# A two-layer hybrid decoder step, split into two token halves with the MLP of one half traced between the heads of the other

## The chip, the cores and the metric

The kernel runs on one core of a Trainium2 chip. The metric is the device time of one execution in microseconds (us), the median of several.

## The reference

One inference step of two layers for a prompt of 1024 tokens and eight sample tokens that attend to paged caches; the 1032 tokens share the weights. Model width 1024, MLP width 4096, all in float32.

```python
D_MODEL = 1024; SEQ = 1024; DEC_BATCH = 8; PAST_LEN = 512; D_FF = 4 * D_MODEL
def _diff_attn(q1, q2, ...):            # layer 0, heads A (4): differential attention
    p = probs(q1, k1) - lam * probs(q2, k2)
    return jnp.einsum('bhqk,bkhe->bqhe', p, v)
def _hgrn2_chunk(S, xs): ...            # layer 0, heads B (4): gated recurrence in chunks
def _fox_attn(q, fq, q_pos, k, v, fk, k_pos):   # layer 1, heads C (8): forgetting attention
    s = einsum(q, k) * DH_C ** -0.5 + fq - fk   # fq, fk: running sums of log forget gates
    p = softmax(where(mask, s, NEG)); return p @ v
def _mlstm_chunk(carry, xs): ...        # layer 1, heads D (4): recurrence with state C, n, m
...
# each layer: h = rmsnorm(x); heads(h @ w_in) ; x += heads @ w_out
#             x += relu(rmsnorm(x) @ w_up) ** 2 @ w_down ;   at the end a last rmsnorm
```

Both prompt heads are causal: a token needs only tokens before it, in attention and in the two recurrences. For the eight samples, heads A and C gather K, V (and for C the log forget values) of 512 past rows each through a page table, 4 pages of 128 rows; heads B and D take a state from memory and write a new one.

## The kernel before

Activations lie with the features on the 128 partitions and tokens along the free axis, so a projection is a weight block of 128 output features (`wh`, `wl`) against a block of tokens. Each float32 product is made of three TensorE matmuls of hi and lo parts (`mm3`, L119: `wh`·`xh`, `wh`·`xl`, `wl`·`xh`) over 8 or 4 blocks of 128 input features. The 1032 tokens are three blocks of 344 (`TB`), so a weight block of 1024 input features costs 72 matmuls and one of 512 (output projection and down projection) 36. `wsplit` brings each weight block once: one DMA on SyncE's queue into `wr` (L97), ScalarE copies it rounded into `wh` (L98), GpSimd subtracts into `wl` (L99). Each of `wr`, `wh`, `wl` has two buffers.

The program is traced in the order of the layers. Stage by stage, in the profile's time: input projection of the first heads; four diff heads with the other input projections as `fill` between their pieces; HGRN heads with the output projection as `fill`; the rest of the output projection and the whole MLP of layer 0 with six accumulators (793 to 1506); gates and projections of layer 1; eight fox heads with fill; mLSTM with the output projection as fill; the MLP of layer 1 (2197 to the end). `tick` hands out `fill` (dense work) and `back` (the samples' work) at a rate per piece of a head. In the head stages of diff and fox the dense work has one accumulator bank of PSUM (`acc1`, `acc4`), in HGRN and mLSTM two.

The framework's list scheduler fixes the order on each engine when the program is built; on the chip each engine takes its instructions in that order. Priority is the order of the trace.

The sample's work of layer 1 (`fox_sample`) is a chain: rows of q to DRAM and back as broadcasts (`dq`), 32 gathers of K pages (`dk`) with a multiply on GpSimd and a sum on VectorE each, 32 gathers of log forget values (`lgg`, copied to `lg` by GpSimd), a softmax, its probabilities through DRAM (`ps_c`, `pse`), then 32 gathers of V pages with a broadcast matmul (`selb`) and a VectorE reduction each. Before, it stands as `back` beside the fox heads, from head 2 on. `mlstm_sample` (`vrow_d`, `vb`, `Cs`, `qsd`) stands beside the mLSTM chunks.

Of the kernel before, what the change touches and what calls it, by code (L numbers as in the profile page):

```python
# [10 lines left out]
F32 = mybir.dt.float32  # L11
# [11 lines left out]
TB = 344  # L23
NTB = T // TB
# [31 lines left out]
class Step:  # L56


    def __init__(self, tc, ctx, I, O):
# [7 lines left out]
        self.A = ent(tc.tile_pool(name="A", bufs=1))  # L67
# [9 lines left out]
        self.idb = cp.tile([128, 128], BF16, name="idb")  # L77
        self.tri = cp.tile([128, 128], BF16, name="tri")
        self.rb = cp.tile([128, T], F32, name="rb")

        self.xs = self.dr.tile([128, KC, T], F32, name="xs")
        self.os = [self.dr.tile([8, 128, T], F32, name=f"os{i}") for i in range(2)]

    def pool(self, st, name, bufs=1, psum=False):
        kw = dict(space=bass.MemoryType.PSUM) if psum else {}
        return st.enter_context(self.tc.tile_pool(name=name, bufs=bufs, reuse_waits="tile", **kw))
# [35 lines left out]
    def project(self, ps, src, evict, m=128, w=None):  # L122

        h, l = w or self.wsplit(src, KC, m)
        for tb in range(NTB):
            sl = slice(tb * TB, (tb + 1) * TB)
            pt = ps.tile([128, 512], F32, name="acc", tag="acc")
            self.mm3(pt[:m, :TB], h, l, self.xh, self.xl, range(KC), sl, m)
            evict(pt[:m, :TB], sl)
            yield  # L130

    def project_rms(self, ps, src, evict, rms, w=None):

        h, l = w or self.wsplit(src, KC)
        pts = []
        for tb in range(NTB):
            pts.append(ps.tile([128, 512], F32, name="acc", tag="acc"))
            self.mm3(pts[tb][:, :TB], h, l, self.xh, self.xl, range(KC), slice(tb * TB, (tb + 1) * TB))
        rms()
        for tb in range(NTB):  # L140
            evict(pts[tb][:, :TB], slice(tb * TB, (tb + 1) * TB))

    def project_to(self, pool, ps, src, dst, scale=None, keep=None, done=None):

        nc = self.nc
        z = pool.tile([128, T], F32, name="z", tag="z", bufs=2)
        yield from self.project(ps, src, self.scaled(z, scale))
        if keep is not None:
            nc.gpsimd.tensor_copy(keep, z[:, NP:])
        nc.sync.dma_start(dst, z[:])  # L150
# [25 lines left out]
    def scaled(self, dst, scale=None):  # L176

        nc, rb = self.nc, self.rb
        m = dst.shape[0]

        def ev(p, sl):
            if scale is None:
                nc.vector.tensor_tensor(dst[:, sl], p, rb[:m, sl], op=ALU.mult)  # L183
            else:
                nc.vector.scalar_tensor_tensor(dst[:, sl], p, scale, rb[:m, sl], op0=ALU.mult, op1=ALU.mult)
        return ev


    def gain(self, x, n, gcol, hi, lo):
# [3 lines left out]
        for sl in [slice(tb * TB, (tb + 1) * TB) for tb in range(NTB)] if n == KC - 1 else [slice(0, T)]:  # L193
# [3 lines left out]
    def sumsq(self, pool, x, n, tags=(("sq", 1), ("ld", 2))):  # L197
        nc = self.nc
        if n == 0:
            self.sq = pool.tile([128, T], F32, name="sq", tag=tags[0][0], bufs=tags[0][1])  # L200
            nc.scalar.activation(self.sq[:], x, AF.Square)
        else:
            t = pool.tile([128, T], F32, name="sqt", tag=tags[1][0], bufs=tags[1][1])
            nc.scalar.activation(t[:], x, AF.Square)
            nc.vector.tensor_tensor(self.sq[:], self.sq[:], t[:], op=ALU.add)  # L205

    def rms(self, pool, ps, sq=None, t0=0, n=T):

        nc = self.nc
        sq = self.sq if sq is None else sq  # L210
        full, rest = divmod(n, 128)
        pt = ps.tile([128, 512], F32, name="acc", tag="acc")
        for c in range(full + 1):
            w = min(128, n - 128 * c)
# [3 lines left out]
        for w, cs in ((128, slice(0, full)), (rest, slice(full, full + 1))):  # L218
            nc.vector.tensor_scalar(v[:w, cs], pt[:w, cs], 1.0 / D, EPS, op0=ALU.mult, op1=ALU.add)
        h = pool.tile([128, 9], F32, name="rp", tag="rp")  # L220
        nc.gpsimd.memset(h[:], -0.5)
        nc.gpsimd.tensor_tensor(v[:, :full + 1], v[:, :full + 1], h[:, :full + 1], op=ALU.pow)
        for g in range(0, full + 1, 4):
            pt = ps.tile([128, 512], F32, name="acc", tag="acc")
            for j, c in enumerate(range(g, min(g + 4, full + 1))):
                w = min(128, n - 128 * c)
                d = pool.tile([128, 128], F32, name="rd", tag="rd", bufs=2)
                nc.vector.tensor_scalar(d[:, :w], self.ident[:, :w], v[:, c:c + 1], None, op0=ALU.mult)
                nc.tensor.matmul(pt[:, 128 * j:128 * j + w], lhsT=self.ones[:], rhs=d[:, :w], start=True, stop=True)  # L229
            w = min(512, n - 128 * g)  # L230
            nc.scalar.copy(self.rb[:, t0 + 128 * g:t0 + 128 * g + w], pt[:, :w])


    def head_norm(self, sm, po, pm, dst, gcol, gate, n, eps=None, thr=None):

        nc = self.nc
        sq = sm.tile([128, 512], F32, name="hsq", tag="hsq")
# [3 lines left out]
        rs = sm.tile([128, 512], F32, name="hrs", tag="hrs")  # L241
# [11 lines left out]
    def hgrn_gates(self, ph, ps, pr, first):  # L253

        nc, I = self.nc, self.I
        self.fS = self.dr.tile([4, 128, T], F32, name="fS")
        self.gS = self.dr.tile([4, 128, T], F32, name="gS")
# [12 lines left out]
        for h in range(4):  # L270
            z = ph.tile([128, T], F32, name="z", tag="z", bufs=2)
            if h:
                self.now(self.project(ps, I["w_in_e"][16 + h], self.scaled(z)))
            else:
                self.project_rms(ps, None, self.scaled(z), lambda: self.rms(ph, pr), w=first)
# [3 lines left out]
            nc.sync.dma_start(self.fS[h], g[:])  # L279
        for h in range(4):  # L280
            z = ph.tile([128, T], F32, name="z", tag="z", bufs=2)
            self.now(self.project(ps, I["w_in_e"][24 + h], self.scaled(z)))
# [3 lines left out]
            nc.sync.dma_start(self.gS[h], g[:])  # L286
# [10 lines left out]
    def hgrn_unit(self, h, u, ph, ps):  # L297
# [7 lines left out]
        us = slice(N * u, N * u + N)  # L305
        t512 = lambda name, bufs: ph.tile([128, N], F32, name=name, tag=name, bufs=bufs)
        c3 = lambda ap: ap.rearrange("p (c t) -> p c t", t=128)
        f, q, it = t512("hf", 4), t512("hq", 6), t512("hi", 2)
        nc.sync.dma_start(f[:], self.fS[h, :, us])
        nc.sync.dma_start(q[:], self.qbS[h, :, us])  # L310
        nc.sync.dma_start(it[:], self.ibS[h, :, us])
        k = t512("hk", 5)
        nc.scalar.activation(k[:], f[:], AF.Copy, scale=-1.0, bias=1.0)
        yield
        ir = ph.tile([128, nch, 128], F32, name="hir", tag="hir", bufs=6)
# [5 lines left out]
        AT = ph.tile([128, nch, 128], F32, name="hA", tag="hA", bufs=6)  # L321
# [7 lines left out]
        pe, pes = f[:], ph.tile([128, N], F32, name="hpe", tag="hpe", bufs=5)  # L329
# [27 lines left out]
        nc.sync.dma_start(gt[:], self.gS[h, :, us])  # L357
        yield
        S = ph.tile([128, nch - 1, 128], F32, name="hS", tag="hS", bufs=3)
        end = ph.tile([128, 128], F32, name="hE", tag="hE", bufs=4)  # L360
# [22 lines left out]
        nc.sync.dma_start(self.os[0][4 + h][:, us], ot[:])  # L383
        self.half_done += u == 0
# [15 lines left out]
    def hgrn_sample(self, ph, ps):  # L400

        nc, I, O = self.nc, self.I, self.O
        for t, src in ((self.qb_s, self.qbS), (self.ib_s, self.ibS), (self.fb_s, self.fS), (self.gb_s, self.gS)):
            nc.sync.dma_start(t[:].rearrange("p (h b) -> p h b", b=NS), src[:, :, NP:].rearrange("h p b -> p h b"))
        pt = ps.tile([128, 512], F32, name="pm", tag="m")
        nc.tensor.transpose(pt[:32, :128], self.ib_s[:], self.ident[:])
        ri = ph.tile([32, 128], F32, name="ri", tag="row32", bufs=2)
# [1178 lines left out]
```

## Time and profile before

| | |
|---|---|
| time, median of 3 runs | 2920.72 us (2918.53 to 2924.51) |
| profiled execution | 2922.06 us, of it 2920.2 us from the first to the last instruction |
| TensorE busy | 2789.4 us, 17340 matmuls, mean granted clock 0.969 |
| VectorE / ScalarE / GpSimd busy | 1279.9 / 893.0 / 787.4 us |
| DMA | 261.5 MB, mean 90 GB/s |

A matmul's busy time overlaps with the next one's, so the pace of TensorE is read from the distance of starts or from a chain of many matmuls. An idle time is what no matmul covers; a granted clock of 0.5 in a stretch is the lower of its two levels.

### The profile page before, as it was taken

The numbers are of one execution on the slowest core, as the hardware profiler recorded it, in microseconds if no ns is written. First come the engines' busy times: TensorE is split into PE (matmuls) and PEld (weight loads), VectorE is DVE, ScalarE is ACT, GpSimd is POOL, SyncE is SP. The second block draws the span as 40 slices with busy tenths as digits, with TensorE's granted clock in tenths as the row PEclk, the third lists the DMA queues.
The fourth block names the chain that finished last, engine by engine and source line by source line (L and its number), as shares of the span: only waits on it lengthen the run. The fifth ranks groups of instructions, "written<-read, shape, count | busy, mean of one in ns | idle before, by whom it ended". The sixth has DMA issues, their size and how long they took to land.

```text
span 2920.2 us, 43534 instructions
## 1 busy us (share of the span) xinstructions
PE 2789.4 (96%) x17340; PEld 2652.7 (91%) x17340; DVE 1279.9 (44%) x2499; ACT 893.0 (31%) x1548; POOL 787.4 (27%) x640
## 2 busy tenths in 40 slices
PE   8999899799999999999999989889999999999997
PEld 8988777698999999999999988777889999999997
DVE  5144855575622333223344546474453333223335
ACT  4143343212522222222232524353342222222223
POOL 2321720254322222222222244211242222221222
PEclk9999999799999999999999999988999999999998
DMA  3253653542211111111133443644331111111121
GB/s 141 96 162 104 185 143 122 170 124 81 76 55 44 40 47 49 54 47 37 55 116 126 129 142 110 153 143 135 104 98 48 37 48 51 51 48 37 47 62 66
DMA packets 149868, 261.50 MB, mean 90 GB/s; under 512 B 24358, under 2 KB 69190, under 8 KB 149666
## 3 DMA queue, kind: packets, MB, share of 16 engines
q1 hardware_dynamic: 149410, 258.64, 29.3%
q8 instruction: 137, 2.24, 0.3%
q0 software_dynamic: 256, 0.08, 0.2%
q14 instruction: 65, 0.53, 0.1%
HBM read 209.75 MB, written 48.92 MB: 89 GB/s over the span
## 4 chain that ended last, share of the span: by engine, by line
PE 82%; DMA 5%; DVE 5%; issue 4%; POOL 1%; ACT 1%; SPq 1%; DVEq 0%; POOLq 0%; ACTq 0%
PE acc L119 71%; PE po L573 2%; PE S L520 1%; PE S L517 1%; PE pm L557 1%; PE pm L338 1%; DMA dI<-irow 1%; DVE xl L195 1%; DMA kd<-out_ka 1%; DVE sq L205 1%; PE hms L240 1%; DMA kd<-out_kc 0%; DMA ol<-os 0%; PE pm L710 0%; PE acc L229 0%
## 5 line engine op out<-in xcount | busy, mean ns | idle before, releaser
L119 PE MATMUL acc<-xh,wh 128*128 128x344 f32 (+1 forms) x2808 | 915.1, 327 | 28.2 <-DVE z L183 17.1
L119 PE MATMUL acc<-xl,wh 128*128 128x344 f32 (+1 forms) x2808 | 906.9, 323 | 0.6 <-DVE xl L195 0.5
L119 PE MATMUL acc<-xh,wl 128*128 128x344 f32 (+1 forms) x2808 | 899.9, 322 | 3.8 <-POOL wl L99 3.8
L99 POOL TENSOR_TENSOR wl<-wr,wh 128x512 fp32r<-128x512 f32 (+1 forms) x284 | 504.1, 1775 | 1414.3 <-ACT wh L98 1413.6
L119 PEld LDWEIGHTS acc<-xh,wh 128*128 128x128 f32 (+1 forms) x2808 | 534.1, 190 | 39.9 <-DVE z L183 19.6
L119 PEld LDWEIGHTS acc<-xh,wl 128*128 128x128 f32 (+1 forms) x2808 | 532.4, 190 | 6.3 <-POOL wl L99 4.6
L119 PEld LDWEIGHTS acc<-xl,wh 128*128 128x128 f32 (+1 forms) x2808 | 533.7, 190 | 3.3 <-DVE xl L195 1.6
L98 ACT ACTIVATE wh<-wr 128x512 fp32r<-128x512 f32 (+1 forms) x284 | 228.2, 804 | 982.4 <-PE acc L119 843.9
L119 PE MATMUL acc<-ul,wh 128*128 128x344 f32 (+1 forms) x1568 | 495.8, 317 | 0.1
L119 PE MATMUL acc<-uh,wl 128*128 128x344 f32 (+1 forms) x1568 | 494.0, 317 | 1.5 <-POOL wl L99 1.5
L119 PE MATMUL acc<-uh,wh 128*128 128x344 f32 (+1 forms) x1568 | 493.2, 317 | 1.7 <-ACT wh L98 1.7
L1267 DVE TENSOR_TENSOR x<-acc,x 128x344 f32<-128x344 f32 x336 | 173.3, 516 | 438.3 <-PE acc L119 438.3
L119 PEld LDWEIGHTS acc<-uh,wh 128*128 128x128 f32 x1568 | 294.1, 188 | 2.2 <-ACT wh L98 2.1
L119 PEld LDWEIGHTS acc<-uh,wl 128*128 128x128 f32 x1568 | 293.7, 188 | 2.1 <-POOL wl L99 2.1
L119 PEld LDWEIGHTS acc<-ul,wh 128*128 128x128 f32 x1568 | 294.6, 188 | 0.6 <-DVE ul L1202 0.5
L1254 DVE TENSOR_TENSOR ul<-u,uh 128x344 fp32r<-128x344 f32 x192 | 146.1, 763 | 201.8 <-ACT uh L1253 201.8
L1251 DVE SCALAR_TENSOR_TENSOR t<-acc,rb 128x344 f32<-128x344 f32 x192 | 98.5, 516 | 268.1 <-PE acc L119 266.2
L1252 ACT ACTIVATE u<-t 128x344 f32<-128x344 f32 x192 | 93.8, 490 | 323.5 <-DVE t L1251 322.5
L183 DVE TENSOR_TENSOR z<-acc,rb 128x344 f32<-128x344 f32 x138 | 69.9, 512 | 207.6 <-PE acc L119 191.2
L539 ACT ACTIVATE e<-S,st 128x128 f32<-128x128 f32 (+7 forms) x128 | 94.4, 739 | 95.3 <-DVE st L537 42.7
L545 ACT ACTIVATE Ph<-pm 128x512 fp32r<-128x512 f32 (+1 forms) x120 | 64.8, 551 | 110.0 <-PE pm L557 109.1
L1253 ACT ACTIVATE uh<-u 128x344 fp32r<-128x344 f32 x192 | 94.0, 491 | 5.8
(385 smaller groups left out, 3259.0 us busy)
## 6 DMA issues: line engine op xcount, KB each, us to landing
wr<-in_w_up SPq DMA_DIRECT2D x64, 512.0 KB
wr<-in_w_down SPq DMA_DIRECT2D x128, 256.0 KB
wr<-in_w_in_e SPq DMA_DIRECT2D x27, 512.0 KB
wr<-in_w_out SPq DMA_DIRECT2D x48, 256.0 KB
wr<-in_w_in_o SPq DMA_DIRECT2D x24, 512.0 KB
x<-in_x SPq DMA_DIRECT2D x16, 516.0 KB
qd<-qS SPq DMA_DIRECT2D x32, 256.0 KB
dk<-in_cache_k_a SPq DMA_DIRECT2D x32, 256.0 KB
```

The lines of the kernel that those rows point to most:

```text
L98: nc.scalar.activation(h[:, :kk, :m], r[:, :kk, :m], AF.Copy)
L99: nc.gpsimd.tensor_tensor(l[:, :kk, :m], r[:, :kk, :m], raw(h[:, :kk, :m]), op=ALU.subtract)
L119: nc.tensor.matmul(out, lhsT=w[:, k, :m], rhs=a[:, sl], start=(n == 0), stop=(n == last))
L183: nc.vector.tensor_tensor(dst[:, sl], p, rb[:m, sl], op=ALU.mult)
L539: nc.scalar.activation(e[:, :L], S[:, :L], AF.Exp, bias=st[:, 0:1], scale=-1.0, accum_out=st[:, 1:2])
L545: nc.scalar.activation(ph[:, :n], pt[:, :n], AF.Copy)
L573: nc.tensor.matmul(o[:, 128:] if half else o, lhsT=w, rhs=parts[x][:, c:c + (128 if half else 256)], start=(j == 0 and n == 0), stop=(j == ...
L1251: nc.vector.scalar_tensor_tensor(t[:], pt[:, :TB], 0.0, self.rb[:, sl], op0=ALU.max, op1=ALU.mult)
L1252: nc.scalar.activation(u[:], t[:], AF.Square)
L1253: nc.scalar.activation(H[:, sl], u[:], AF.Copy)
L1254: nc.vector.tensor_tensor(L[:, sl], u[:], raw(H[:, sl]), op=ALU.subtract)
L1267: nc.vector.tensor_tensor(x[:, sl], pt[:, :TB], self.x[n][:, sl], op=ALU.add)
```

## The change

The tokens are two halves of 512 and 520 (`HW`), and blocks are one of 512 columns for half 0, two of 260 for half 1. The output projection, the MLP and layer 1's input projection of a half are one generator, `half()`, which yields after each block; the run traces a half's generator as `fill` between the heads of the other half. The sequence is: first projections for both halves; HGRN heads of half 0 with the remaining projections; diff heads of half 0; diff heads of half 1 and HGRN heads of half 1, with layer 0's `half(0, 0)` and the samples of diff and HGRN; then for each half u of layer 1: input projection, fox heads, mLSTM, with `half(0, 1)` between those of half 0 and `half(1, 0)` between those of half 1; last `half(1, 1)` alone. The weights of `half()` and of layer 1's input are therefore loaded and split twice. `fox_sample` moves from beside the fox heads to half 1's mLSTM stage, ahead of `mlstm_sample`. The dense work in the head stages has two accumulator banks (`accM`). The second score matmul of diff reads all 128 partitions instead of 64.

```diff
-TB = 344
-NTB = T // TB
+HW = (NP // 2, T - NP // 2)
+BLOCKS = (((0, 512),), ((0, 260), (260, 260)))
...
+    def half(self, layer, u, ps, pr, tp, alone=False):
...
+        for part in range(2):
...
+            for f in range(KC):
...
+                h, l = self.wsplit(I["w_out"][layer, part, f], 4)
+                for o, m in blocks:
+                    pt, sl = acc(), slice(o, o + m)
+                    self.mm3(pt[:, :m], h, l, oh, ol, range(4), sl)
+                    nc.vector.tensor_tensor(x[f][:, sl], pt[:, :m], x[f][:, sl], op=ALU.add)
+                    yield
...
+        for cc in range(8):
...
+                h, l = self.wsplit(I["w_up"][layer, 4 * cc + f], KC)
...
+                h, l = self.wsplit(I["w_down"][layer, cc, f], 4)
...
         if fox is None:
-            q2, k2 = Q1[hi], K2[hi]
+            K2 = hd.tile([128, nk], F32R, name="K2", tag="K2", bufs=2)
+            nc.gpsimd.tensor_tensor(K2[:], kd[:], raw(K1[:]), op=ALU.subtract)
+            q2, k2 = Q1, K2
...
-            pS, pm, acc = self.pool(st, "pS4", 2, True), self.pool(st, "pm4", 2, True), self.pool(st, "acc4", 1, True)
...
-                    self.back = (66 / 24, [self.fox_sample(hd, pm, pS)])
...
-            self.fill = (32 / 70, [self.out_a(1, ph, acc, self.xs), self.out_b(1, ph, acc)])
-            self.back = (10 / 48, [self.mlstm_sample(ph, pm, qkv)])
...
+            accM = self.pool(st, "accM", 2, True)
...
+            self.fill = (1.7, [self.half(0, 0, accM, accM, M)])
...
+                self.diff_half(1, hd, pm, pS)
...
+                self.fill = (1.4, self.fill[1])
+                self.back = (76 / 60, [self.hgrn_sample(ph, pm, pS), self.diff_sample(ph, pm, pS)])
+                self.hgrn_half(1, ph, pm, 3, 5)
...
+            for u in range(2):
...
+                    self.fill = (0, [self.half(u, 1 - u, accM, accM, M)])
...
+                self.fill = ((5.0, 2.4)[u], self.fill[1])
...
+                    self.fox_half(u, hd, pm, pS)
+                self.fill = ((1.7, 1.4)[u], self.fill[1])
...
+                    if u:
+                        self.back = (76 / 30, [self.fox_sample(ph, pm, pS), self.mlstm_sample(ph, pm, pS, qkv)])
+                    self.mlstm_prompt(u, ph, pm, qkv)
+                    self.drain("back")
...
+            self.now(self.half(1, 1, ps, pr, tp, alone=True))
```

How the change moves instructions, at three places. First TensorE at the end of the fox heads. Before, the last heads' scores (`S`, L517, L519, L520), transposes (`pm<-ident`, L557) and products with V (`po`, L573) and the sample's broadcasts (`selb`, L710) follow one another:

```order
L710 MATMUL pm<-PP,selb 128x512
L557 MATMUL pm<-ident,e 128x128 x4
L573 MATMUL po<-Ph,VV_18707 128x256
L557 MATMUL pm<-ident,e 128x128 x4
L573 MATMUL po<-Pl,VV_18707 128x256
L573 MATMUL po<-Ph,VV_18707 128x256
L573 MATMUL po<-Pl,VV_18707 128x256
L557 MATMUL pm<-ident,e 128x128 x3
L573 MATMUL po<-Ph,VV_18707 128x256
L517 MATMUL S<-K_19000,Q_18999 128x384
```

After the change the last head of half 1 stands among dense matmuls (L121, 512 columns):

```order
L598 MATMUL po<-Ph,VV_21302 128x256
L598 MATMUL po<-Ph,VV_21302 128x128
L121 MATMUL acc<-uh,wh 128x512
L598 MATMUL po<-Pl,VV_21302 128x128
L598 MATMUL po<-Pl,VV_21302 128x256
L121 MATMUL acc<-ul,wh 128x512
L121 MATMUL acc<-uh,wl 128x512
```

The dense work that had run out in this place before now lies between the pieces.

Second SyncE's queue at the gathers of the log forget values. Each gather is a DMA with five control rows around it. Before, weight loads (`wr`) and stores stand between every few of them:

```order
L653 DMA lgg<-in_cache_logf_c 128x8
L647 TENSOR_LOAD pages
L647 ISA x2
L97 DMA wr<-in_w_in_o 128x1024
L653 ISA
L653 DMA lgg<-in_cache_logf_c 128x8
L1130 DMA os_84<-ft 64x512
```

After the change 25 of the 32 follow one another (the last two and what comes behind are shown), with no weight load among them:

```order
L676 DMA lgg<-in_cache_logf_c 128x8
L670 TENSOR_LOAD pages
L670 ISA x2
L676 ISA
L676 DMA lgg<-in_cache_logf_c 128x8
L670 TENSOR_LOAD pages
L670 ISA x2
L99 DMA wr<-in_w_down 128x512 x4
```

The four weight loads behind them are the next that TensorE's dense work needs.

Third TensorE at the end of the mLSTM sample (`qsd`, `Cs`, L1054 before, L1095 after). Before, its matmuls lie in groups of four between output projection and chunks:

```order
L119 MATMUL acc<-oh_19510,wl 128x344
L1054 MATMUL pm<-qsd,Cs 128x1 x4
L934 MATMUL pm<-ident,mvt 128x128 x4
L940 MATMUL pm<-ident,mk_19443 128x128
L940 MATMUL pm<-ident,mk_19444 128x128
L972 MATMUL pm<-mvr,mP 128x129 x4
L1054 MATMUL pm<-qsd,Cs 128x1 x4
L119 MATMUL acc<-oh_19507,wh 128x344
```

After the change they stand in one piece, and `half(1, 1)`, which has the 260-column matmuls, begins behind them:

```order
L733 MATMUL pm<-PP,selb 128x512
L1061 MATMUL pm<-w_24643,sel 128x16 x2
L682 MATMUL pm<-ident,vsd 32x128
L1066 MATMUL pm<-ed,ones 128x32
L1040 MATMUL pm<-ident,mh 128x128 x4
L1095 MATMUL S<-qsd,Cs 128x1 x32
L1098 MATMUL S<-qn,ones 128x16 x2
L1108 MATMUL pm<-hsd,ident 128x32
L254 MATMUL hms<-hsq,ones 128x32
L121 MATMUL acc<-uh,wh 128x260
```

No dense matmul is left between the last broadcast of the fox sample (`selb`) and the end of the mLSTM sample.

In the order after the change, 279 dense matmuls of 512 columns stand between the first matmul of the fox sample (a transpose of `qc_s`) and the `hms` above: 207 of them ahead of its softmax's scores, 72 behind; 142 rows of other matmuls stand among them. The stages with heads and fill (HGRN and diff of both halves; fox and mLSTM of each half) hold 3,724 dense matmuls of 512 columns and 2,210 of 260. Over the whole program, 4,728 dense matmuls have 512 columns and 9,456 have 260; before, the same 14,184 products were in three blocks of nearly always 344.

## Rows read from the trace of the kernel before

**Rows 1.** The page: busy time, share of the span and count of each engine.

```profile
PE 2789.4 (96%) x17340; PEld 2652.7 (91%) x17340; DVE 1279.9 (44%) x2499; ACT 893.0 (31%) x1548; POOL 787.4 (27%) x640
```

**Rows 2.** Stretches, all work: length, busy time of each engine, clock, DMA share, GB/s.

```profile
150.00:722.00 572.00, 525.02 (x3054) 456.22 (x3054) 343.85 (x779) 189.58 (x346) 188.20 (x172) 0.93 0.46 136
1590.00:2122.00 532.00, 484.08 (x2968) 428.74 (x2967) 283.81 (x631) 207.66 (x416) 149.97 (x176) 0.93 0.47 134
1865.00:1924.00 59.00, 58.52 (x382) 54.61 (x380) 33.08 (x78) 25.76 (x49) 11.10 (x12) 1.00 0.45 136
1924.00:1987.00 63.00, 51.88 (x261) 38.72 (x260) 42.97 (x97) 33.88 (x70) 2.90 (x11) 0.84 0.36 114
2122.00:2197.00 75.00, 71.66 (x470) 67.19 (x470) 45.10 (x65) 34.13 (x46) 30.69 (x22) 1.00 0.30 93
```

**Rows 3.** Chain that ended last: start, length, what, count; two dense pieces.

```profile
738.42 8.91 PE acc L119 x72
...
793.78 710.91 PE acc L119 x4512
```

**Rows 4.** Stretches, L119 alone: length, PE busy (count), weight loads, clock, DMA, GB/s.

```profile
150.00:722.00 572.00, 282.18 (x1528) 254.67 (x1528) 0.93 0.46 136
1590.00:2122.00 532.00, 275.11 (x1530) 250.30 (x1529) 0.93 0.47 134
1865.00:1924.00 59.00, 39.89 (x228) 36.13 (x226) 1.00 0.45 136
1924.00:1987.00 63.00, 0.08 (x1) 0.00 (x0) 0.84 0.36 114
```

**Rows 5.** TensorE's timeline between two dense blocks in the fox stage.

```profile
1677.42 0.31 PE L119 MATMUL acc<-xh,wl 128*128 128x344 f32 x1
1678.34 0.43 PE L119 MATMUL acc<-xh,wh 128*128 128x344 f32 x1 [0.61 <-DVE z L183]
```

**Rows 6.** TensorE's timeline: scores of a diff head; output projection with 512 columns.

```profile
204.73 0.50 PE L520 MATMUL S<-K,Q 64*128 64x512 f32 x1
205.16 0.44 PE L517 MATMUL S<-K,Q 128*128 128x384 f32 x1
...
705.06 0.39 PE L119 MATMUL acc<-ob,wl 128*128 128x512 f32 x1
705.29 0.40 PE L119 MATMUL acc<-ob,wh 128*128 128x512 f32 x1
```

**Rows 7.** Groups with shapes apart: busy us, mean ns, idle before, releaser.

```profile
L99 POOL TENSOR_TENSOR wl<-wr,wh 128x512 fp32r<-128x512 f32 x168 | 220.0, 1310 | 794.2 <-ACT wh L98 793.8 <-PE acc L119 0.4
L98 ACT ACTIVATE wh<-wr 128x512 fp32r<-128x512 f32 x168 | 105.8, 631 | 555.9 <-PE acc L119 534.8 <-issue 17.6 <-POOL wl L99 2.2
```

**Rows 8.** ScalarE's copies L98 from 2122 to 2146: what ended its idle times.

```profile
  PE acc L119: 8.3, 5
  DMA wr<-in_w_out: 0.5, 1
```

**Rows 9.** fox_sample, multiplies, copies, V reductions: ns min/median/max, first and last start.

```profile
L684 POOL TENSOR_TENSOR dk<-dk,dq x32: 1253/1288/1647, 1718.0 to 1785.3; 128x512 f32<-128x512 f32 x32
...
L1146 POOL COPY lg<-lgg x32: 192/198/424, 1786.5 to 1824.0; 128x8 f32<-128x8 f32 x32
...
L712 DVE CUSTOM_DVE_ANT_0 dk<-dk,pm x31: 668/681/689, 1857.7 to 1958.8; 128x512 f32<-128x512 f32 x31
```

**Rows 10.** Chain, fox and mLSTM sample: start, length, what.

```profile
1806.23 0.33 SPq L653
1807.39 0.33 SPq L653
...
1839.91 7.42 DMA ps_c<-de
1848.26 7.87 DMA pse<-ps_c
...
2019.78 5.13 DMA vb<-vrow_d
```

More of the change, by code (lines that the diff above doesn't have):

```diff
@@ new lines, in project_to @@
+    def project_to(self, pool, ps, src, dst, us=(0, 1), scale=None, keep=None):
+        nc = self.nc
+        t0, t1 = HS[us[0]].start, HS[us[-1]].stop
+        z = pool.tile([128, t1 - t0], F32, name="z", tag="z", bufs=2)
+        ev = self.scaled(z, us, scale)
+        h, l = self.wsplit(src, KC)
+        for u in us:
+            for _ in self.project(ps, None, ev, (u,), w=(h, l)):
+                yield
+            nc.sync.dma_start(dst(u), z[:, HS[u].start - t0:HS[u].stop - t0])
+        if keep is not None and t1 == T:
+            nc.gpsimd.tensor_copy(keep, z[:, NP - t0:])
@@ L835, in mlstm_rows @@
[L835 to L847 removed]
+        rs = slice(128 * h, 128 * h + 128)
@@ L908, in mlstm_prompt @@
[L908 to L913 removed]
+            pt = ps.tile([128, 512], F32, name="pm", tag="m")
+            nc.tensor.matmul(pt[:], lhsT=self.sel2[:, i, :], rhs=wi[:], start=True, stop=True)
+            nc.vector.tensor_tensor(qw[i][:], q[i][:, :512], pt[:], op=ALU.mult)
@@ new lines, in half @@
+            if cc == 7:
+                break
+            for f in range(KC):
+                h, l = self.wsplit(I["w_down"][layer, cc, f], 4)
+                for o, m in blocks:
+                    pt, sl = acc(), slice(o, o + m)
+                    self.mm3(pt[:, :m], h, l, uh, ul, range(4), sl)
+                    nc.vector.tensor_tensor(x[f][:, sl], pt[:, :m], x[f][:, sl], op=ALU.add)
+                    yield
+        if alone:
+            self.finish(tp, ps, pr, u, x, uh, ul, wd)
+            return
@@ new lines, in half @@
+        while layer == 0 and self.inp is None:
+            yield "wait"
+        ih, il, sq = [], [], None
+        for f in range(KC):
+            h, l = self.wsplit(I["w_down"][layer, 7, f], 4)
+            for o, m in blocks:
+                pt, sl = acc(), slice(o, o + m)
+                self.mm3(pt[:, :m], h, l, uh, ul, range(4), sl)
+                nc.vector.tensor_tensor(x[f][:, sl], pt[:, :m], x[f][:, sl], op=ALU.add)
+                yield
+            if layer == 0:
+                nc.sync.dma_start(self.xs[u][:, f, :], x[f][:, :n])
+                ih.append(self.inp.tile([128, n], F32R, name=f"ih{f}"))
+                il.append(self.inp.tile([128, n], F32R, name=f"il{f}"))
+                self.gain(x[f], f, C_MIX + 8, u, ih[f], il[f])
+            sq = self.sumsq(mp, x[f][:, :n], f, sq)
```

919 lines of the change are left out of this document (454 added, 465 removed).

## The prediction

> **What bounds the kernel now.** I read the page first: TensorE is busy for 2789.4 of 2920.2 us [rows 1], so only its work or its waits can give time back. Next the chain: from 793.78 on 4,512 dense matmuls take 710.91 us, 157.6 ns each [rows 3]. The two MLPs run at that pace without waiting, so nothing is to be had there. Then the stretches. The head stages, 150 to 722 and 1590 to 2122, are 1104 us long with TensorE idle for 47.0 and 47.9 us, and a granted clock of 0.93 [rows 2]; 7% of 1104 is 77 us that the lower of the two clock levels took. Together 172 us. The timeline shows that idle time is under-reported: between two dense blocks the starts are 0.92 us apart where the pace is 0.16, so 0.76 is lost and 0.61 shown, while the only bank is emptied by `z` [rows 5]. Scaling the 95 us by that quarter gives 119, and 196 us lost in all, 18% of these stages.
>
> What do they depend on? L119 counted alone has 1,528 and 1,530 matmuls there [rows 4], at 157.6 ns 482 us, 44% of the time. Where dense work is 61% (228 matmuls in 59 us, 1865 to 1924), 0.5 us is idle at full clock, a loss of 1%; where there is none (1924 to 1987) 11.1 us is idle and the clock is 0.84, a loss of about a third [rows 2, 4]. Waits of heads are lost when the fill is thin or has run out. That is what the change moves.
>
> **The sum.** Dense work: a weight block took three blocks of 344, 472.7 ns per product of 128 by 128; now one of 512 and two of 260. 512 columns start 0.23 us apart [rows 6]. For 260 a line through the two paces gives 121 ns, the chain of 72 gives 123.8 with whatever it waited [rows 3]. So 0.23 + 2×0.121 is 472 ns, no change; with 123.8 it is +5 ns, over 4,728 products +23 us. I take +10 (0 to +23); this also stands for the doubled weight stream, of which below.
>
> Scores: 64-row matmuls of 512 columns are followed after 0.43 us, where 128 rows take 0.23 [rows 6]. By the order there are 48 of 512 columns and 48 of fewer; 96 by about 0.19 saved is −18. The 32 additional transposes of V, at about 0.22, cost 7. Together −11 (−18 to 0).
>
> Joints: where heads ended and the MLP began, 3.3 of 75 us are idle [rows 2]; two such joints now lie beside heads: −6 (−8 to 0).
>
> Head stages: their other work is 1104 − 196 − 482 = 426 us, 415 after the line above. By the order, 3,724 × 0.23 + 2,210 × 0.121 = 1124 us of dense work stand there, 73% of 1539. That is above the 61% stretch, with two banks, but holds over a much longer time, with each head's loads and set-up twice. From 1% (that stretch) to 10% (halfway to today's 18%) I take 4%: 62 us lost instead of 196, −134 (−181 to −42).
>
> The new hole: `fox_sample` now stands at the end, and `half(1, 0)` does not last as long as it. Its chain worked out: q rows to DRAM and back 8 us (as `ps_c`, 7.4 [rows 10]); the K multiplies 41 at GpSimd's 1.29 each, 69 as they ran before (1718.0 to 1786.6), I take 55 [rows 9]; then copies of log forget values, the last 37 us after the last multiply [rows 9], which is also 32 gathers at SyncE's 1.16 apart [rows 10]; softmax with two trips through DRAM, 7.4 and 7.9 [rows 10], some 18; V 37 at the gathers' pace, up to 60, I take 50 (101 before, spread by its rate [rows 9]); `mlstm_sample`, eight states in two buffers, four rounds of `vb` at 5.1 [rows 10] and about 1.5 of arithmetic, with a trip for its rows and its tail 35 (30 to 45). Sum 203 us (169 to 237). Beside it TensorE has 279 dense matmuls, 65 us, and 142 rows of other work, an estimate of 45: 110. What is left is a wait of 93 us; I take +90 (59 to 127). What is late next: 25 gathers in a row on SyncE take 29 us, and the weight loads behind them (`in_w_down`) come that much later, so dense work can't fill the time; on TensorE everything queues behind the waiting scores, then behind `S<-qsd,Cs`, and `half(1, 1)` begins only after the `hms` that follows.
>
> The moved gathers of layer 0 I cost at nothing: diff and HGRN samples have over 200 us of dense work and four head units beside them. Without that cover their chain is as long as the one above, less the log forget values.
>
> Sum against the profiled execution: 2922 + 10 − 11 − 6 − 134 + 90 = 2871; the median of the runs is 1.3 below it, so I say **2870**.
>
> The weight stream: a 256 KB block now serves 12 × 0.23 = 2.8 us of TensorE instead of 5.7. Copy and subtraction take 0.63 and 1.31 [rows 7]; with two `wr` buffers a load may take 5.6 − 0.63 − 1.31 = 3.6 us before TensorE waits. From 2122 on the output projection already ran at one block per 2.9 us; ScalarE waited there five times for TensorE (8.3 us) and once for the load (0.5) [rows 8]. So on a quiet memory it is hidden. The Trainium skill's "DMA: Bandwidth & Descriptors", section "Anatomy of one DMA", speaks against halving what a load serves: each DMA has a fixed part of about 2.0 us that does not shrink with its size. By its formula 256 KB is 2.6 us (an estimate from that page), below the 3.6, and the dense term would be 0 and the sum 2861.
>
> **The rivals.** *The hole is covered.* If K runs at GpSimd's pace and V at the gathers', the wait is 59, and with 1% of loss the head stages give 181: 2922 + 10 − 11 − 6 − 181 + 59 = 2793, with single terms between 2780 and 2830. For it: the 61% stretch. Against: 25 gathers in a row.
>
> *The weight stream becomes the bound (slower).* Place: dense blocks of 512 words per partition in the mixed stages, where the DMA share is 0.46 [rows 2], against 0.30 in the stretch of rows 8. If a load takes 4.4 us there, two weights need 6.3 instead of 5.6, 0.37 us for each of 320 such blocks, +119 us at most: 2870 + 119 is about 2990, half of it 2930. It decides from 3.6 us on. For it: GpSimd gets about 400 us more of subtractions (144 more of 512 words at 1.31 [rows 7], 88 of twice that), and a `wl` stuck behind a sample's multiplies delays TensorE. The Trainium skill's "GPSIMD Engine Reference", section "Specifications", adds that GpSimd shares its SBUF interfaces with VectorE, with contention where a VectorE instruction has two inputs there. The multiplies' median and maximum, 1.29 and 1.65 [rows 9], would fit that. Against: rows 8, and that head work in between gives loads more time.
>
> *The waits belong to the heads, not to thin fill (slower).* Twice the units with shorter pieces wait twice as often; if 10% of 1539 is lost, −42 instead of −134: 2963. For it: 44% of dense work does not keep 18% from being lost today. Against: the single bank is gone.
>
> *It doesn't do what it says.* The scheduler could have pulled dense work together ahead of the heads, and gain and hole cancel: 2916 to 2927. The order, which has dense rows between head pieces, speaks against it.
>
> **How the numbers follow.** Chances: the sum 0.50 (own range 2830 to 2915), the covered hole 0.24 (2780 to 2830), the weight stream 0.10, waiting heads 0.10, no change 0.06. The range leaves out the upper part of the two slower cases and a little below: 2775 to 2945. A measurement can tell about 0.2%, 6 us, from no change. Faster 0.73 (nearly all of the first two), same 0.07, slower 0.20.
>
> **What would show it.** Right: stretches with heads have TensorE idle under 3% and clock near 1; the only large idle stretch lies between the fox sample's scores and the first 260-column matmul of `half(1, 1)`, 60 to 130 us, ended by `lg`, VectorE's `ov` and `Cs`; dense pieces at 0.23 and 0.12. Wrong: TensorE waiting for `wl` or `wh` all through mixed or dense stretches (the stream); idle time spread evenly over heads, ended by `e`, `K` or `z`; a hole under 50 us; or a second hole at layer 0's samples.

## The result and the profile after

The change made the kernel slower: 3017.36 us median (3012.77 to 3025.16) against 2919.62, ratio 1.0335, interval 1.0310 to 1.0361, about 98 us. The forecast was 2870, faster, with 2945 as the upper end.

The page of the changed kernel, the engines' busy time and share of a span of 3010.8 us, answers to [rows 1]; its mean granted clock is 0.950:

```profile
PE 2780.6 (92%) x17375; PEld 2471.2 (82%) x17376; DVE 1416.0 (47%) x2617; ACT 1081.7 (36%) x1899; POOL 1214.5 (40%) x911
```

TensorE is idle for 230.2 us where it was 130.8. The clock deficit (the time multiplied by the missing share of the clock) is 5.0% of the span, 151 us, where it was 3.1%, 89 us. The two overlap: 57 of the 151 us and 19 of the 89 lie in idle times, by the trace's records of the granted clock, and a low clock costs nothing there. Counted once, 324 us are lost where 202 were, 123 more; the span grew by 91, so some 32 us of TensorE's own time were saved. GpSimd is busy for 427 us more, ScalarE for 189.

Five stretches of the changed kernel (columns as in [rows 2]): layer 0's HGRN heads of half 1 with two samples; dense work; fox heads of half 1; the end of them and mLSTM with two samples; `half(1, 1)` alone.

```profile
742.00:1068.00 326.00, 277.50 (x1285) 226.01 (x1283) 167.21 (x284) 83.96 (x133) 173.59 (x139) 0.89 0.52 155
1500.00:1725.00 225.00, 220.86 (x1810) 217.99 (x1809) 88.82 (x164) 80.16 (x145) 93.31 (x58) 1.00 0.33 98
1960.00:2300.00 340.00, 340.00 (x1697) 284.60 (x1697) 158.47 (x233) 164.75 (x270) 130.40 (x77) 1.00 0.31 89
2300.00:2560.00 260.00, 179.64 (x789) 134.45 (x788) 119.00 (x270) 55.29 (x109) 114.35 (x152) 0.77 0.54 153
2560.00:2920.00 360.00, 355.38 (x2911) 350.90 (x2910) 144.33 (x267) 126.76 (x227) 151.35 (x93) 1.00 0.31 91
```

The fox heads without a sample beside them run as I had hoped: nothing idle in 340 us, full clock. The two stretches with samples lose most: 48.5 us idle and 11% clock deficit (36 us, 11 of them in idle time) in the first, 80.4 idle and 23% (60 us, 29 of them in idle time) in the second. And the dense stretches, which had lost 0.3 of 713 us, now have 4.1 of 225 and 4.6 of 360 idle.

What TensorE waited for from 742 to 1068 (us, times, longest), first rows:

```profile
PE S L444 <- DVE dS L440: 21.7, 6, 11.9
PE acc L121 <- ACT wh L100: 8.2, 3, 3.4
```

and from 2300 to 2560:

```profile
PE S L1095 <- DVE Cs L1090: 27.4, 8, 5.9
PE acc L121 <- ACT wh L100: 15.1, 4, 7.5
PE S L1206 <- POOL lg L1186: 14.1, 2, 13.7
PE pm L1040 <- POOL mh L1034: 4.6, 1, 4.6
PE pm L991 <- DVE ov L735: 4.0, 1, 4.0
```

The states of the mLSTM sample (`Cs`), weight copies, and the log forget values (`lg`) stand first; the HGRN sample's states (`dS`) make a second hole in layer 0. The chain in time through the last stretch (start, length, what):

```profile
2343.25 5.61 DMA dq<-qrow_c
...
2364.90 5.45 DMA wr<-in_w_down
...
2382.73 5.87 DMA wr<-in_w_up
...
2421.85 3.13 DMA lgg<-in_cache_logf_c
...
2450.26 7.44 DMA dk<-in_cache_v_c
...
2518.62 4.62 DMA vb<-vrow_d
2523.38 0.63 POOL vb L1089
2524.03 0.44 DVE Cs L1090
2524.49 3.71 DMA out_scd<-Cs
```

It is the chain of the prediction, and its pieces came near the forecast (in brackets): from the first matmul of the fox sample (2338) to the `hms` (2556) 218 us (203), of them the K multiplies 56 (55), the log forget values 37 (37), V 55 (50) and the mLSTM sample 44 (35). TensorE is idle for 75 of the 218 us. At the end stands a link that I left out: a state's buffer is free only when the new state is stored (`out_scd`, 3.7), so a round of two states takes about 9.6 us, not 6.6.

### The profile page after: what moved, and what is told of

It is laid out like the page before. It is cut to its first block, busy times and chain, and to the rows that moved or that the text cites. A ratio compares the mean times of both kernels' runs of the same rounds, so it can differ in the third digit from the quotient of the medians.

```text
span 3010.8 us, 45736 instructions
## 1 busy us (share of the span) xinstructions
PE 2780.6 (92%) x17375; PEld 2471.2 (82%) x17376; DVE 1416.0 (47%) x2617; ACT 1081.7 (36%) x1899; POOL 1214.5 (40%) x911
## 5 line engine op out<-in xcount | busy, mean ns | idle before, releaser
L101 POOL TENSOR_TENSOR wl<-wr,wh 128x512 fp32r<-128x512 f32 (+2 forms) x517 | 904.4, 1752 | 1305.1 <-ACT wh L100 1208.9
L100 ACT ACTIVATE wh<-wr 128x512 fp32r<-128x512 f32 (+2 forms) x517 | 411.8, 799 | 1185.1 <-PE acc L121 836.5
L121 PE MATMUL acc<-uh,wh 128*128 128x260 f32 (+1 forms) x2080 | 674.0, 329 | 35.2 <-ACT wh L100 16.0
L121 PE MATMUL acc<-ul,wh 128*128 128x260 f32 (+1 forms) x2080 | 665.9, 323 | 0.8 <-DVE ul L1242 0.5
L121 PE MATMUL acc<-xh,wh 128*128 128x260 f32 (+1 forms) x1760 | 589.5, 336 | 26.5 <-ACT wh L100 12.4
L121 PE MATMUL acc<-uh,wl 128*128 128x260 f32 (+1 forms) x1856 | 595.7, 329 | 3.1 <-POOL wl L101 2.8
L121 PE MATMUL acc<-xl,wh 128*128 128x260 f32 (+1 forms) x1760 | 587.0, 334 | 3.5 <-DVE xl L207 3.4
L121 PE MATMUL acc<-xh,wl 128*128 128x260 f32 (+1 forms) x1760 | 584.5, 334 | 1.7 <-POOL wl L101 1.6
L121 PEld LDWEIGHTS acc<-uh,wh 128*128 128x128 f32 x2080 | 398.2, 192 | 73.2 <-ACT wh L100 22.4
L121 PEld LDWEIGHTS acc<-ul,wh 128*128 128x128 f32 x2080 | 398.9, 192 | 28.9 <-DVE ul L1242 2.5
L121 PEld LDWEIGHTS acc<-xh,wh 128*128 128x128 f32 x1760 | 335.3, 190 | 60.8 <-ACT wh L100 14.4
L121 PEld LDWEIGHTS acc<-uh,wl 128*128 128x128 f32 x1856 | 351.4, 192 | 35.1 <-POOL wl L101 6.7
L121 PEld LDWEIGHTS acc<-xh,wl 128*128 128x128 f32 x1760 | 334.1, 190 | 35.8 <-POOL wl L101 4.4
L121 PEld LDWEIGHTS acc<-xl,wh 128*128 128x128 f32 x1760 | 335.6, 191 | 34.0 <-DVE xl L207 4.3
L121 PE MATMUL acc<-ih,wl 128*128 128x260 f32 (+2 forms) x600 | 189.8, 319 | 4.0 <-POOL wl L101 3.9
L121 PE MATMUL acc<-il,wh 128*128 128x260 f32 (+2 forms) x600 | 189.6, 318 | 0.0
L121 PE MATMUL acc<-ih,wh 128*128 128x260 f32 (+2 forms) x600 | 189.4, 319 | 0.0
```

What stands on the lines that cost most here:

```text
L100: nc.scalar.activation(h[:, :kk, :m], r[:, :kk, :m], AF.Copy)
L101: nc.gpsimd.tensor_tensor(l[:, :kk, :m], r[:, :kk, :m], raw(h[:, :kk, :m]), op=ALU.subtract)
L121: nc.tensor.matmul(out, lhsT=w[:, k, :m], rhs=a[:, sl], start=(n == 0), stop=(n == last))
```

## The experiments

Ratios are to the kernel before on the same chip, with 95% intervals; the changed kernel's is 1.0335. 1% is 29 us.

**Without samples, and where the fill goes.** First theory: the holes beside the samples are what was lost. Rivals: the doubled weight stream, and halved heads.

The changed kernel without the four sample parts:

```diff
-                self.back = (76 / 60, [self.hgrn_sample(ph, pm, pS), self.diff_sample(ph, pm, pS)])
+                self.no_sample(ph, 0)
...
-                        self.back = (76 / 30, [self.fox_sample(ph, pm, pS), self.mlstm_sample(ph, pm, pS, qkv)])
+                        self.no_sample(ph, 1)
```

> The changed kernel with the work of all four sample parts left out (HGRN, diff, fox, mLSTM samples; their outputs are not computed and the samples' head outputs are set to one). About 25 us of TensorE's own work goes with them. Theory 1: the losses beside them, 126 us from 2300 to 2560 and most of 79 us from 742 to 1068, go too: 2790 to 2860. Rival 2: only a little beyond the 25 us, 2940 to 2990. Rival 3: the same as rival 2.

Measured 0.9670 (0.9642 to 0.9697), 2814 us: the samples cost 6.65%, 194 us, in the changed kernel. That looked like the first theory.

The kernel before with its MLP weights loaded and split twice:

```diff
+                    if tb == 2:
+                        h, l = self.wsplit(I["w_up"][layer, 4 * cc + n], KC)
...
+                    if tb == 2:
+                        h, l = self.wsplit(I["w_down"][layer, cc, n], 4)
```

> The kernel before, with every up and down weight block of the MLP loaded and split a second time ahead of the third token block: the doubled weight stream alone. Theory 1 (the samples' chains, standing where the fill runs out, hold TensorE and SyncE's queue): at most +20 us, 2920 to 2940, since the MLP stages have GpSimd and ScalarE half idle. Rival 2 (the doubled weight stream costs the time): +60 us or more, 2980 and up, with TensorE waiting for wh and wl in 793 to 1506. Rival 3 (halved heads wait twice as often): no change, as theory 1.

Measured 1.0132 (1.0103 to 1.0161), +38 us: between the two. Its first MLP as a stretch of 740 us (columns as in [rows 2]):

```profile
800.00:1540.00 740.00, 728.34 (x4599) 724.47 (x4598) 278.41 (x401) 246.58 (x387) 314.12 (x195) 1.00 0.30 95
```

and the first row of TensorE's waits in it (us, times, longest):

```profile
PE acc L119 <- ACT wh L98: 8.9, 8, 2.1
```

11.7 us are idle, where 0.3 of 713 were, with GpSimd busy only 42% of the time: short waits at the start of a block, about 1 us each, one per group of four up and eight down blocks, no engine full.

Fill of half 1 of layer 1 handed out later:

```diff
-                self.fill = ((5.0, 2.4)[u], self.fill[1])
+                self.fill = ((5.0, 1.6)[u], self.fill[1])
...
-                self.fill = ((1.7, 1.4)[u], self.fill[1])
+                self.fill = ((1.7, 3.5)[u], self.fill[1])
```

> The changed kernel with the fill of layer 1's half 1 handed out later: rate 1.6 instead of 2.4 beside the fox heads, 3.5 instead of 1.4 beside mLSTM, so about 100 us of dense work moves to where the fox sample runs. Theory 1: the hole from 2300 on shrinks by 40 to 80 us and the fox stage loses 10 to 20: 2950 to 2995. Rival 2: no change within 10 us. Rival 3: slower, since the fox heads have less fill, 3030 to 3060.

Measured 1.0335 (1.0302 to 1.0369): no gain. The edit moved less than the expectation says: from the fox sample's first matmul to the `hms`, 340 dense matmuls stand where 279 stood (14 us more), 172 of them ahead of the softmax's scores (207 before the edit). The stretch takes 230 us instead of 218, with 78 idle instead of 75. TensorE's first two waits from 2300 to 2560 (us, times, longest) were still there:

```profile
PE S L1095 <- DVE Cs L1090: 26.5, 8, 8.2
PE S L1206 <- POOL lg L1186: 18.5, 2, 18.1
```

More fill did not shorten a wait that stands ahead of it in TensorE's order.

The mLSTM sample ahead of the fox sample:

```diff
-[self.fox_sample(ph, pm, pS), self.mlstm_sample(ph, pm, pS, qkv)]
+[self.mlstm_sample(ph, pm, pS, qkv), self.fox_sample(ph, pm, pS)]
```

> The changed kernel with the mLSTM sample traced ahead of the fox sample instead of behind it; the work is the same. Theory 1: the 40 us at the end in which TensorE waits for one state after another (S from qsd, Cs) moves to where dense work is still there: 2975 to 2995. Rivals 2 and 3: no change within 10 us.

Measured 1.0433 (1.0403 to 1.0464): 28 us slower. The waits for the states shrank to 1.6 us, but the fox sample's last broadcast came at 2570 us instead of 2511, and `half(1, 1)` begins behind it.

**The other side of the samples.** The kernel before without the four parts (the same edit):

> The kernel before with the work of all four sample parts left out (their outputs are not computed; the samples' head outputs of two parts are set to one): the other side of the run without samples. The changed kernel lost 194 us that way, against the changed kernel itself. Theory 1 (the samples' chains cost far more in the new places than in the old ones): 30 to 80 us less than before, 2830 to 2880, so that without samples the halves are the faster kernel, ratio to before about 0.98. Rivals 2 and 3 (weight stream, halved heads): the samples cost as much here, so 2700 to 2760 and the halves stay the slower kernel.

Measured 0.9421 (0.9404 to 0.9439), 2742 us. The samples cost 5.79%, 169 us, there as well. The first theory fell: their new places explain only 194 − 169 = 25 of the 98 us (give or take 12, by the three intervals). Without samples the halves are still 2.49% slower, 72 us. The page of this kernel:

```profile
PE 2681.6 (98%) x17084; PEld 2581.4 (94%) x17084; DVE 1170.0 (43%) x2239; ACT 885.5 (32%) x1527; POOL 660.3 (24%) x470
```

Its two head stages, begun and ended at the same instructions as those of [rows 2], all work (same columns):

```profile
150.00:637.00 487.00, 472.54 (x2946) 419.51 (x2944) 281.51 (x658) 183.82 (x333) 126.90 (x114) 0.99 0.33 106
1505.00:1933.00 428.00, 423.22 (x2808) 391.14 (x2807) 234.28 (x488) 203.30 (x405) 82.64 (x60) 0.98 0.37 113
```

The same stretches, L119 alone (columns as in [rows 4]):

```profile
150.00:637.00 487.00, 269.23 (x1538) 244.47 (x1536) 0.99 0.33 106
1505.00:1933.00 428.00, 258.44 (x1508) 240.41 (x1507) 0.98 0.37 113
```

In 915 us 19 are idle and 15 are clock deficit, a loss of 4%. The same count gives 172 of 1104 us, 16%, with the samples [rows 2]. The dense work is the same, 3,046 matmuls for 3,058; since the stages are shorter, its share rises from 44 to 52%. A straight line between the prediction's two points (18% lost at a share of 44%, 1% at 61%) would leave about 10% at 52%, an estimate. The undivided heads with one accumulator bank did not wait much: TensorE's waits for the evicted bank (`z`), 19.8 us in the two stages with samples, are 2.2 us in the whole kernel without. The samples beside the heads made TensorE wait.

**Single places in the samples.** Log forget gathers beside the fox heads:

```diff
+                    if u:
+                        self.back = (2.0, [self.fox_logf()])
                     self.fox_half(u, hd, pm, pS)
+                    self.drain("back")
```

> The changed kernel with the 32 gathers of log forget values traced beside the fox heads of half 1 instead of between the K and the V gathers of the fox sample. Theory 1: SyncE's run of 25 gathers (29 us) leaves the chain, and the weight loads behind it come earlier: 20 to 40 us less than the changed kernel, ratio 1.020 to 1.027. Rivals 2 and 3: no change within 8 us, ratio 1.031 to 1.036.

Measured 1.0233 (1.0207 to 1.0258): 30 us less, as expected, about the 29 us of 25 gathers.

HGRN states one by one among the K pages:

```diff
-[self.hgrn_sample(ph, pm, pS), self.diff_sample(ph, pm, pS)]
+[self.mixed(self.hgrn_sample(ph, pm, pS), self.diff_sample(ph, pm, pS))]
```

> The changed kernel with the HGRN sample's eight states handed out one after every third page of the diff sample's K phase instead of all ahead of it. Theory 1: TensorE's waits for the states (21.7 us at S from qb_s, with 24 us of low clock beside) shrink: 15 to 35 us less, ratio 1.022 to 1.029. Rivals 2 and 3: no change.

Measured 1.0310 (1.0288 to 1.0332), −7 us, and the interval touches that of the changed kernel: inconclusive, and less than expected.

> Both of the last two edits, log forget values early and HGRN states spread. Theory 1: the two gains add, 35 to 75 us less than the changed kernel, ratio 1.009 to 1.022. Rivals: no change.

Measured 1.0207 (1.0182 to 1.0232): 37 us, the sum of the two, at the low end.

**What is left without samples.** Three runs on the changed kernel without samples (0.9670). The second reading of the weights left out:

```diff
-                h, l = self.wsplit(I["w_up"][layer, 4 * cc + f], KC)
+                h, l = self.again(I['w_in_o'][0], KC) if u else self.wsplit(I["w_up"][layer, 4 * cc + f], KC)
```

(and the same for the output projection, the down projection and layer 1's input projection.)

> The changed kernel without samples, with the second reading of the weights left out too: half 1's output projections, MLPs and layer 1's input projection use one block that stays in SBUF, so half 1's results are wrong and its matmuls as many as before; DMA, ScalarE and GpSimd have the kernel before's number of weight blocks. Without samples the ratio to the kernel before was 0.967 for the halves and 0.942 for the undivided kernel: 72 us to be explained. Rival 2 (the doubled weight stream): 30 to 70 us of them, ratio 0.943 to 0.957. Rival 3 (halved heads and halved stages wait more): nothing of them, 0.963 to 0.968.

Measured 0.9497 (0.9476 to 0.9519): 1.73%, 50 us. The doubled weight stream is the largest part of the 72.

The norms replaced by a constant:

```diff
-        rms = lambda: self.rms(mp, pr, sq, self.rb[u], n)
+        rms = lambda: nc.gpsimd.memset(self.rb[u][:, :n], 0.01)
```

> The changed kernel without samples, with the RMS norm's result left out in the middle of each half's MLP path and ahead of layer 1's input projection (a constant stands in; the squares are still summed, the small matmuls and the waits for them are gone). There are six such norms where the undivided kernel has three. A form of rival 3 (each half ends in a chain on which everything waits): 20 to 45 us less, ratio 0.952 to 0.960. Rival 2: less than 10 us, 0.963 to 0.968.

Measured 0.9548 (0.9531 to 0.9564): 1.22%, 36 us for six norms. The undivided kernel keeps three of its own, so about half is what the halves add. That half is an estimate; no run left out the undivided kernel's three. One of these joints, in TensorE's timeline of the changed kernel without samples:

```profile
969.14 0.40 PE L121 MATMUL acc<-uh,wl 128*128 128x512 f32 x1
975.66 1.87 PE L229 MATMUL acc<-ones,sq 128*128 128x1 f32 x8 [6.12 <-DVE sq L219]
981.26 0.80 PE L121 MATMUL acc<-uh,wh 128*128 128x260 f32 x2 [3.74 <-ACT uh L1246]
```

After the last down block VectorE still has a residual sum, the lo part and a sum of squares to do for the last features before `sq` is complete; TensorE waits 6.1 us, then 3.7 for the other half's `uh`, and nothing is ahead in its order.

> Both of the last two, on the changed kernel without samples. If weight stream and norms are the cause together, the gap to the undivided kernel without samples closes: ratio 0.935 to 0.948. If heads that wait because they are halved are the cause: 0.958 to 0.966.

Measured 0.9327 (0.9309 to 0.9345), a little below the range: 100 us less than 0.9670, where the two alone gave 50 and 36, and 27 less than the undivided kernel without samples (which has its own three norms). Weight stream and norms close the gap in time. That does not rule out waits of halved heads: the change also saves TensorE work, and TensorE is still idle for 73.0 us at a clock of 0.988 here, against 55.4 at 0.990 in the undivided kernel without samples, some 20 us more lost. Two places stand out, 14.1 us idle from 400 to 500 (diff heads of half 0) and 8.0 from 2255 to 2295 (the last norm of half 0, a seventh that stayed in).

**One part of the change alone, on the kernel before:** 128 rows in the diff heads' second score matmul.

```diff
-            q2, k2 = Q1[hi], K2[hi]
+            K2 = hd.tile([128, NP], F32R, name="K2", tag="K2", bufs=2)
+            nc.gpsimd.tensor_tensor(K2[:], kd[:], raw(K1[:]), op=ALU.subtract)
+            q2, k2 = Q1, K2
```

> The kernel before with one part of the change alone: the second score matmul of the diff heads reads all 128 partitions. The prediction's term is -18 us: 96 matmuls, each about 0.19 us shorter. If TensorE is what ends there: 10 to 20 us less than before, ratio 0.993 to 0.9965. If the diff stage waits for other things: no change, 0.998 to 1.002.

Measured 0.9904 (0.9886 to 0.9922), 2884.64 us: −28 us, beyond the expected 10 to 20 and the −18 of the sum, and faster than both kernels. The sum priced only the 64-row matmul. In the kernel before, the 128-row matmul ahead of it is slowed too:

```profile
204.31 0.49 PE L517 MATMUL S<-K,Q 128*128 128x512 f32 x1
204.73 0.50 PE L520 MATMUL S<-K,Q 64*128 64x512 f32 x1
205.16 0.44 PE L517 MATMUL S<-K,Q 128*128 128x384 f32 x1
```

The next start comes after 0.42 us, and in the median of 45 such places after 0.41; where another 128-row matmul follows, after 0.24. In the changed kernel both are followed after 0.23 us:

```profile
460.31 0.39 PE L545 MATMUL S<-K,Q 128*128 128x512 f32 x1
460.54 0.39 PE L542 MATMUL S<-K,Q 128*128 128x512 f32 x1
```

**What of the samples costs so much.** Page numbers fixed when the kernel is built, so SyncE loads no register from the page table (other rows of the pools are gathered). The edit also takes away the rule that a gather's register load waits for the gather before it, in lines that are not shown here:

```diff
-        self.last_gather = nc.sync.dma_start(dst, pool[bass.ds(page, 1), :, :].rearrange("o p f -> (o p) f")).ins
+        nc.sync.dma_start(dst, pool[n % 32:n % 32 + 1, :, :].rearrange("o p f -> (o p) f"))
```

> The changed kernel with the page numbers of the gathers fixed when it is built, so SyncE no longer loads a register from the page table for each of the 160 gathers (the rows gathered are the wrong ones; their bytes and DMAs are as many). If the samples' price is SyncE's pace of about 1.15 us per gather, behind which weight loads queue: 50 to 110 us less than the changed kernel, ratio 0.997 to 1.017. If it is the length of the chains (DMA landings, GpSimd multiplies, states in two buffers): less than 20 us, 1.027 to 1.035.

Measured 1.0250 (1.0230 to 1.0271), −25 us.

> The same edit on the kernel before. Pace of the gathers: 40 to 100 us less, ratio 0.966 to 0.986. Length of the chains: less than 20 us, 0.993 to 1.001.

Measured 0.9937 (0.9921 to 0.9954), −18 us. The first lies between its two expectations, the second inside the lower one. The gathers of V pages of the fox sample start 0.48 us apart (median) in both, where it was 1.11 in the changed kernel and 1.14 in the kernel before. With the rule gone the scheduler also moved the log forget gathers in among the K pages of the changed kernel and ahead of most of them in the kernel before, so the −25 us hold that move too (−30 us alone, above). SyncE's pace is a small part in both.

The kernel before with 128 rows and the log forget gathers ahead of the fox sample:

```diff
-            self.fill, self.back = (3.2, qkv), (0, [])
+            self.fill, self.back = (3.2, qkv), (5.0, [self.fox_logf(hd)])
```

> The kernel before with the two single edits that paid: 128 rows in the diff heads' second score matmul (0.990 alone) and the log forget gathers traced beside the first two fox heads, ahead of the sample's K phase. If the 37 us of these gathers stand in the chain that runs the fox stage dry: another 10 to 25 us, ratio 0.982 to 0.987. If not: 0.989 to 0.992.

Measured 0.9899 (0.9882 to 0.9916), 2882.62 us: no more than the 128 rows alone. Where the gathers stand among weight loads they cost nothing that this shows; it is the changed kernel that had made them a cost.

State samples (HGRN, mLSTM) left out of the kernel before, and of the changed one:

```diff
-            self.back = (8 / 84, [self.hgrn_sample(ph, pm)])
+            self.no_state(ph, 0)
...
-            self.back = (10 / 48, [self.mlstm_sample(ph, pm, qkv)])
+            self.no_state(ph, 1)
```

> The kernel before with the HGRN and mLSTM samples' work left out (their outputs are not computed, their head outputs set to one); the two samples that gather pages stay. All four together cost 169 us here. If the chains of states and their stores are the larger part: 80 us or more less, ratio below 0.973. If the paged samples are: 20 to 50 us less, 0.983 to 0.993.

Measured 0.9889 (0.9869 to 0.9910), −32 us: the paged samples are the other 137 of 169.

> The changed kernel with the HGRN and mLSTM samples' work left out. All four samples cost 194 us here. Waits for the states are 21.7 us (HGRN) and 27.4 us (mLSTM) in its trace, with low clock beside them. If the chains of states are the larger part here: 80 us or more less, ratio below 1.006; if the paged samples are: 30 to 70 us less, 1.010 to 1.024.

Measured 1.0122 (1.0102 to 1.0141): 2.13%, 62 us; the paged samples are the other 132 of 194. So the paged ones cost about the same in both, and the 25 us that the samples cost more come from the states: 62 against 32 (the intervals leave some 11 us on this difference).

GpSimd's multiplies of the K phase left out of the kernel before:

```diff
-                nc.gpsimd.tensor_tensor(kt[:, j, :], kt[:, j, :], qb[:], op=ALU.mult)
```

> The kernel before with the 64 GpSimd multiplies of the paged samples' K phase left out (the sums are then of K alone, a wrong result): 84 us less of GpSimd, everything else stays. If GpSimd's hold, on which weight splits wait, is what the paged samples cost: 30 us or more less, ratio below 0.99. If not: 0.994 to 1.002.

Measured 0.9906 (0.9886 to 0.9927), −27 us of 137: between the two expectations, close to the 30 us. If that adds to the page table's 18, some 90 us of the paged samples are not traced to a single thing.

## Why the prediction was wrong

**The step that failed** is "Head stages", −134 us. It laid the 172 us of [rows 2] to thin fill, since a stretch with 61% of dense work lost 1% and one with none a third, and scaled that to 73%. The views gave only a correlation, and the 172 counts 11 us of low clock in idle times twice. Without samples the same undivided heads with the same single bank lose 4%, at a dense share of 52%, so most of the loss was the samples'. Those were moved, not taken away: in the changed kernel they cost 194 us for 169. There was little to recover, and the −134 went to nothing.

**The hole** was the right mechanism in the right place: a wait at the scores, one at V, one at the states, ended by `lg`, `ov` and `Cs`, with weight loads late behind 25 gathers. Its chain took 218 us, inside the 169 to 237 of the sum (whose low end adds to 171). From 2300 to 2560 it is 80 us idle (forecast 93), and 31 more by a low clock outside idle times, which the sum had no term for. The run with early gathers took 30 us from it; the states' part was longer by the stores. But as a term of +90 beside −134 it was counted against a gain that wasn't there: part of the same work had cost as much in the old place, so the net price of all moved samples is 25 us, and that is the states', with the second hole in layer 0 that "cost at nothing" denied.

**The dense term**, +10 with the weight stream in it, was mis-sized: left out of the halves, the second reading is worth 50 us, beyond the +23 of the bound; added to the undivided kernel, for the MLPs alone, 38. The few blocks of [rows 8] ran almost without a wait, which was no measure for some 230 additional ones that share ScalarE and GpSimd with other work, and the dense stretches now lose 1 to 2%. The fixed part of a DMA that the Trainium skill's "DMA: Bandwidth & Descriptors" names in "Anatomy of one DMA" is given there for DMAs that GpSimd issues; the weight loads go through SyncE's queue. The estimate from it, 2.6 us for 256 KB, fits two such loads in `half(1, 1)` (2.60 and 2.74 us in the chain at 2945 and 2952), but not the one beside samples in the chain above, 5.45 (the 5.87 is of 512 KB). The rival "the weight stream becomes the bound" had the right cause and a form that is only partly seen. Beside samples loads do pass 3.6 us and TensorE waits up to 7.5 us for `wh`. Without samples its waits for `wh` and `wl`

```profile
PE acc L121 <- ACT wh L100: 8.4, 11, 4.1
PE acc L121 <- POOL wl L101: 8.0, 18, 1.7
```

fall from these 16.4 us only to 8.3 when the second reading is left out; its waits for `sq` fall from 17.4 to 8.8 and for `uh` from 9.7 to 3.4. So most of the 50 us is not time in which TensorE waits for a weight, and how the second reading delays the rest no run shows.

**The joints**, −6, had the wrong sign. I counted the idle time at two joints as hidden, and not that halves have six norms where there were three. Half of the 36 us that six cost is about +18, an estimate.

**The scores**, −11 with the transposes, were right in sign and too small: −28 alone, before the transposes' 7. The sum had the 96 matmuls of 64 rows and left out the 128-row matmuls ahead of them, which lost nearly as much each.

In round numbers from the runs: +50 weight stream, +18 norms, +25 samples make 93 of the 98 us. The −28 of the scores is then outweighed by losses of about the same size, which no run here took apart; the some 20 us more that TensorE loses with stream and norms both gone are part of them. The denser fox stretch (nothing idle from 1960 to 2300) is no gain of the halves: without samples the undivided kernel's fox and mLSTM stage is idle for 4.8 of 428 us.

## What to carry to other kernels

A stage that waits while its fill is thin is not thereby waiting for fill: leave the suspected side work out, on the kernel before, and see what the same stage, between the same instructions, loses then. That one run was worth more than the rest of the working here. Idle time and low clock must not be added without taking off what lies in both. When a pass is split, count what is done once per pass (weight loads and their splits, norms and their joints) at its full number, and look for waits that no engine's busy share shows. And on an engine that takes work in order, more fill behind a waiting instruction hides nothing; what helps is to bring the late operand earlier (the gathers, −30 us) or to take work away (128 rows, −28 us: at 0.990 no version here that leaves nothing out is clearly faster).

## What the runs showed of the hardware

Score matmuls of 512 columns that alternate between 64 and 128 rows started 0.43 us (behind the 64-row one) and 0.41 us (behind the 128-row one) apart; where 128 rows followed 128 rows it was 0.24. A 66-row matmul did not have this price: the next start came after 0.24 us. Giving all of them 128 rows was cheaper by 28 us for 96 pairs.

A page number loaded from a table for each gather was not the price of the gathers: with the numbers fixed SyncE issued them 0.48 us apart where it had been 1.11 to 1.14, but that saved only 18 and 25 us for 160 gathers, 0.11 and 0.16 us each, a change of order included.

With the samples gone the mean granted clock of the undivided kernel rose from 0.969 to 0.990. Some 50 of the 169 us that the samples cost there were low clock outside idle times (71 us before, 18 without).
